# Attention over ragged batches: what the one-tile loops wait for, and how their rows are masked

## The chip, the cores and the metric

The kernel runs on one core of a Trainium2 chip, in one launch. The metric is the device time of that core in microseconds (us). Its engines are named as in the profile: PE (TensorE: matmul, PEld its weight loads), ACT (ScalarE), DVE (VectorE), POOL (GpSimd) and SP (SyncE, which issues the DMAs here). The mean granted TensorE clock of the profiled execution was 0.992 of full speed.

## The reference

For each of 32 batch entries, self-attention with 8 heads of 64 over the first `lengths[b]` rows of 512; the rows behind are zero.

```python
scale = 1.0 / np.sqrt(head_dim)
output = np.zeros_like(x)                       # x: 32 x 512 x 512
for b in range(batch):
    seq_len = lengths[b]                        # 64 to 511
    x_b = x[b, :seq_len].copy()
    q, k, v = np.split(np.matmul(x_b, w_qkv), 3, axis=-1)
    ...                                         # to heads x seq_len x 64
    scores = scale * np.matmul(q, k.transpose(0, 2, 1))
    attn = np.exp(scores - np.max(scores, axis=-1, keepdims=True))
    attn = attn / (np.sum(attn, axis=-1, keepdims=True) + 1e-08)
    output[b, :seq_len] = np.matmul(attn, v).transpose(1, 0, 2).reshape(seq_len, dim)
```

The draw is seeded, so the lengths are always the same. Sorted from longest to shortest they begin with 502, 447, 446, 436 and end with 143, 140, 134, 119, 101, 86, 79, 75.

## The kernel before, in words

**Sorted pairs and twelve loops.** The core sorts the lengths on the chip and works on entries in pairs, longest first: 16 pairs. A pair is one iteration, and its two entries are its two positions, `j` = 0 and 1. There are twelve loops, one for each width N in `LOOPS` (512, 448, and 384 down to 96 in steps of 32), and a pair runs in the loop of the smallest width that holds its longer entry. Two loops have one tile of 128 rows (`n == 1`): width 128 and width 96. With these lengths each of them runs one iteration: pair 14 (101 and 86) in the loop of width 128, pair 15 (79 and 75), the last, in the loop of width 96. The text calls their four positions (14,0), (14,1), (15,0) and (15,1).

**Projections ahead.** A position computes the scores, exponentials, products with the values, and the division of its own entry, and between these the projections Q, K and V of the *next* position's entry, whose transposed rows `xT` a DMA has brought. In the last pair's second position there is no next entry. Its projections and their casts have `skip` set (`ends = int(n == 1 and j == 1)`), and `emit_all` puts them behind a branch: while `pair < B // 2 - skip` they run, otherwise an Else part only raises their semaphores, so that whoever counts on them goes on. So in (14,1) they run, and in (15,1) they are skipped. In both parts `issue` first does the step's waits; in the Else part it then raises the semaphore (L1736) where the engine would have run the step.

**An order written by hand.** `ORDER[N]` lists each position's steps. In a loop of one tile, `S0` are all scores (PE, two banks of PSUM, matmuls of line L1240) and their exponentials (ACT, L1258, two instructions: heads 0 to 3, and heads 4 to 7); `Q0`, `K0`, `V0` are the projections (PE, L290 and L301) with their cast out of PSUM (L1373 and L1389; a `*` puts it on ACT, else it is on DVE); `A0` and `A4` are the products with the values for heads 0 to 3 and 4 to 7 (PE, L1417), each followed by its division (`normed`, DVE). The digits behind `@` are the PSUM banks that the step takes. `L` and `P` write masks of live rows, `D` loads rows, `X` transposes them into `xT`.

**The division.** The products' last column is the sum of the exponentials. `normed` emits three DVE instructions for each of A0 and A4: the reciprocal of the sums (R, L1477), its product with the mask of live rows, taken from the column of `v_aug` (U, L1483), and the product of the 128 x 256 results with it into `out_nat` (O, L1486). The position's store (SP, L1096) waits for both O.

**Waits.** `plan_waits` walks through the steps of a loop in their order, with what was left by the loops before, and gives each step the waits that it needs. `clock[engine]` holds what an engine is known to have seen done; a wait teaches it (`learn`), and a later step of the same engine need not wait for it again. So a wait that a skippable projection makes on PE also serves the steps behind it on PE, in both parts of the branch.

Of the kernel before, what the change touches and what calls it, by code (L numbers as in the profile page):

```python
# [11 lines left out]
FP32 = mybir.dt.float32  # L12
# [3 lines left out]
ALU = mybir.AluOpType  # L16
AX = mybir.AxisListType

P = 128
NH = 8  # L20
HD = 64
# [18 lines left out]
def plan_waits(head, bodies, entries, rare):  # L40
# [22 lines left out]
    def follow(chain):  # L63
# [5 lines left out]
        for at, v in enumerate(chain):  # L69
# [10 lines left out]
            for w, j, k, op in todo:  # L80
                b = -1 if v == "head" else 2 * (at - ahead) + (j or 0)
                mine = clock[op.eng]
                older = w != "head" and came < w - 1

                def learn(o):
# [30 lines left out]
                for o in sorted(needs, key=lambda o: -o["order"]):  # L116
# [3 lines left out]
                    if o["entry"]:  # L120
                        wait = ("entry", o["name"])
                    elif o["name"] not in shared:
                        wait = ("head", o["name"])
                    elif v == "head":
                        wait = ("lead", o["name"])
                    elif before and o["name"] in rare:
                        wait = ("iterin", o["name"], first // 2 - o["b"] // 2)
                    elif o["name"] in rare:
                        wait = ("iter", o["name"], b // 2 - o["b"] // 2)
                    elif o["dma"] and before:  # L130
                        wait = ("iterin", o["name"], first // 2 - o["b"] // 2)
                    elif o["dma"]:
                        wait = ("iter", o["name"], b // 2 - o["b"] // 2)
                    elif o["name"] not in has[v] and (not older or ends_in[o["name"]] < v - 2):
                        wait = ("last", o["name"])
                    elif before:
                        wait = ("posold" if older else "posin", o["name"], first - o["b"])
                    else:
                        wait = ("pos", o["name"], b - o["b"])
# [10 lines left out]
                o = {"name": op.name, "by": by, "count": count, "clock": after, "b": b}  # L150
# [21 lines left out]
def kernel(  # L172
# [8 lines left out]
    nc = tc.nc  # L181
    B, MAXS, D = x.shape
# [6 lines left out]
    const = ctx.enter_context(tc.tile_pool(name="const", bufs=1))  # L189
# [8 lines left out]
    def ring(n, shape, dtype, name, pool=const):  # L198
# [15 lines left out]
    alive = const.tile([P, B + 8, NT], FP32)  # L214

    lasts = const.tile([P, B, NT], FP32)
    queries = const.tile([P, 2, NT], F16)
    spare = const.tile([P, 2], F16)

    last_xT = const.tile([P, NC, 3 * P // 2], F16)  # L220
# [51 lines left out]
    }  # L272

    def steps(N, j):
# [4 lines left out]
    def tiles(N):  # L279
        return -(-N // P)  # L280
# [737 lines left out]
    def position(N, j, at, ring):  # L1018
# [4 lines left out]
        n = tiles(N)  # L1023
        n128 = n * P
        gm = {4: 1, 3: 1, 2: 2, 1: 4}[n]
        heads = {4: 1, 3: 2, 2: 2, 1: 4}[n]
# [4 lines left out]
        o = 1 - j  # L1031
        kT, qz, v_aug, o_t = k_bufs[j], q_bufs[j], v_bufs[j], o_bufs[j]
# [4 lines left out]
        def op(*args, **kw):  # L1037
            ops.append(Op(*args, **kw))
# [35 lines left out]
        def unless_past(ahead, name, transfer):  # L1074

            with nc.If_lt(own_pair, (B - ahead - j + 1) // 2):
                last = transfer()
                if last is not None:
                    last.then_inc(sems[name], 16)
            with nc.Else():  # L1080
                nc.sync.sem_inc(sems[name], unit(name))
            nc.end_ifs()
# [45 lines left out]
        def live(table, t0, t1):  # L1128
# [8 lines left out]
                op0=ALU.add,  # L1137
            )

        def live_queries():  # L1140
            return nc.vector.tensor_scalar(
                out=queries[:, :, 0:n],
                in0=alive[:, bass.ds(at("DVE") + j, 2), 0:n],
                scalar1=0.0,
                scalar2=None,
                op0=ALU.add,
            )
# [324 lines left out]
        def normed(h0):  # L1472
            k, pav = sums[h0]
            rcp = r_bufs[k][:, 0 : heads * n].rearrange("p (g t) -> p g t", t=n)

            def reciprocal():
                return nc.vector.reciprocal(out=rcp, in_=pav[:, :, :, HD])  # L1477

            def only_live():
                rows = v_aug[:, 0:n, h0 : h0 + heads, HD].rearrange("p t g -> p g t")  # L1480
                if half_last:
                    rows = queries[:, 1 - j, 0:n].unsqueeze(1).broadcast_to([P, heads, n])
                return nc.vector.tensor_tensor(out=rcp, in0=rcp, in1=rows, op=ALU.mult)  # L1483

            def divide():
                return nc.vector.tensor_tensor(  # L1486
                    out=o_t[:, 0:n, h0 * HD : (h0 + heads) * HD].rearrange(
                        "p t (g d) -> p g t d", d=HD
                    ),
                    in0=pav[:, :, :, 0:HD],  # L1490
                    in1=rcp.unsqueeze(3).broadcast_to([P, heads, n, HD]),
                    op=ALU.mult,
                )

            op(f"R{h0}", "DVE", reciprocal, (f"bk{k}",), (f"r{k}",))
            whose = f"queries{j}" if half_last else f"vl{j}"
            op(f"U{h0}", "DVE", only_live, (f"r{k}", whose), (f"r{k}",))
            op(f"O{h0}", "DVE", divide, (f"bk{k}", f"r{k}"), (f"o{j}.{h0}",))

        def maybe(name, ahead, transfer):  # L1500
            return transfer if n > 2 else lambda: unless_past(ahead, name, transfer)
# [11 lines left out]
        for step in steps(N, j):  # L1513
            step = step.split("@")[0]
            kind, act = step[0], step.endswith("*")
            if kind in "BU":
                name, engines = step[:2], step[4:]
                if name not in opened:
                    opened[name] = (half_qk if kind == "B" else half_values)(name, int(name[1]))
                opened[name](engines)  # L1520
                continue
            num = int(step.strip("*")[1:] or 0)
            if kind == "P":
                op("M", "DVE", pair_mask, (), (f"m{o}",))
                op(
                    "C",
                    "POOL",
                    casts,
                    (f"xn{o}", f"m{o}"),
                    (f"x16{o}",),  # L1530
                    skip=int(n == 1),
                )
                if half_last and j == 0:
                    for b in (1, 0):
                        op(f"Y{b}", "POOL", lambda b=b: gathered(b), (f"xT{b}",), ("lastT",))
            elif kind == "D":
                op(f"LD{j}", "SP", maybe(f"LD{j}", 5, load), (), (f"xn{o}",), dma=True)
            elif kind == "L" and not half_last:
                op("L", "DVE", lambda: live(alive, 0, n), (), (f"vl{o}",))
            elif kind == "L" and j:  # L1540
                op(
                    "L",
                    "DVE",
                    lambda: (live_queries(), live_lasts(), live(alive, 0, n - 1))[2],
                    (),
                    ("vl0", "vlL", "queries0", "queries1"),
                )
            elif kind == "L":
                op("L", "DVE", lambda: live(alive, 0, n - 1), (), ("vl1",))
            elif kind == "S":  # L1550
                scores(num)
            elif kind in "QK":
                qk(step.strip("*"), num, kind == "Q", act)
            elif kind == "V":
                val(step.strip("*"), num, act)
            elif kind == "A":
                av(num)
            elif kind == "Z":
                rest(num)
            elif kind == "W":  # L1560
                last_values(act)
            elif kind == "X":
                transfer = maybe(f"XT{j}", 3, transposed)
                op(f"XT{j}", "SP", transfer, (f"x16{o}",), (f"xT{o}",), dma=True)
# [58 lines left out]
    def at(eng):  # L1623
        return here[eng]
# [78 lines left out]
    for (v, j, k), todo in waits.items():  # L1703
        op = op_of(v, j, k)
# [35 lines left out]
    def issue(v, j, k, op, instead=None):  # L1740
        eng = EN[op.eng]
        for wait in waits[v, j, k]:
            if wait[0] == "head":
                eng.wait_ge(*point[wait[1]])
                continue
            base, amount = value_of(v, j or 0, wait)
            eng.wait_ge(sems[wait[1]], regs[op.eng][base, amount] if base else amount)
        if (op.eng == "SP" or op.name[0] in "YEZ" or op.ahead) and waits[v, j, k]:
            eng.sem_inc(passed, 1)
        if instead:  # L1750
            return instead()
        here["pads"] = [name for name in op.pads if name in sems]
        last = op.emit()
        if v == "head" and op.name in point:
            last.then_inc(point[op.name][0], 16 if op.dma else 1)
        elif op.name in sems and last is not None:
            last.then_inc(sems[op.name], 16 if op.dma else 1)

    with tc.tile_critical():
# [38 lines left out]
        for v, N in enumerate(LOOPS):  # L1798
# [14 lines left out]
            with nc.body(body):  # L1813
# [4 lines left out]
                p = nc.snap(pair, min_val=0, max_val=B // 2 - 1)  # L1818
                here.update({e: p * 2 for e in EN}, pair=p, pairs=pair)
                for j in range(2):  # L1820
                    for e in EN:
                        mine = [(k, op) for k, op in enumerate(bodies[v][j]) if op.eng == e]
# [54 lines left out]
```

## Time and profile before

| | us |
|---|---|
| median of 3 runs (lowest, highest) | 333.87 (333.55, 335.23) |
| the profiled execution's own time | 334.23 |
| its span, first to last instruction | 332.4 |
| busy in the span: PE / ACT / DVE / POOL | 316.7 / 261.7 / 206.5 / 101.9 |

The profiled execution lies 0.36 us over the median, and 1.8 us of its time lie outside its span. Times in the profile are microseconds from the start of the span. A line such as L1486 is a line of the kernel before. In a row of the timeline stand the start, the duration, the engine, line and operation, what is written from what, a count, and in brackets the engine's idle time before with what ended it. "SPq" or "PEldq" is the engine's sequencer: waits, branches and issues.

### The profile page before, as it was taken

To read this page: it belongs to the slowest core of one execution; us is meant where nothing else is said; L and a number is where in the kernel's file an instruction comes from. 1 tells how busy PE (TensorE), PEld (TensorE's weight loads), DVE (VectorE), ACT (ScalarE), POOL (GpSimd) and SP (SyncE) were. 2 spreads that over 40 slices of the span, in tenths; PEclk is the share of its full clock that TensorE was granted. 3 is DMA by queue.
4 is the path that set the end of the run, shared out by engine and by line. 5 is a ranking of instruction groups with operands and counts; after the bars stand their busy time and mean duration, and the time that the engine had idled before them with its cause. 6 is when DMAs were issued, how large, how long until landed. Compare 5 with 4: busy or idle time off the path is not lost.

```text
span 332.4 us, 12738 instructions
## 1 busy us (share of the span) xinstructions
PE 316.7 (95%) x4800; PEld 202.6 (61%) x4800; DVE 206.5 (62%) x670; ACT 261.7 (79%) x402; POOL 101.9 (31%) x148
## 2 busy tenths in 40 slices
PE   7899999999999999999999999999999999999970
PEld 4444645554665556556556666666778776787750
DVE  6666655676776467466565555564676868656572
ACT  5289899878778987978988899789678687888731
POOL 6537040504030330331232143043222334253310
PEclk9999999999999999999999999999999999999996
DMA  7983999399839997686775777649556666666641
GB/s 220 368 302 65 270 192 299 75 338 224 303 52 336 263 212 223 217 248 217 250 240 187 268 212 224 220 178 284 177 156 168 189 184 197 197 195 226 206 146 64
DMA packets 70709, 71.41 MB, mean 215 GB/s; under 512 B 40704, under 2 KB 40704, under 8 KB 70656
## 3 DMA queue, kind: packets, MB, share of 16 engines
q1 hardware_dynamic: 70608, 70.74, 72.1%
q8 instruction: 29, 0.48, 0.6%
q14 instruction: 24, 0.20, 0.2%
q10 hardware_dynamic: 48, 0.00, 0.0%
HBM read 27.80 MB, written 33.55 MB: 185 GB/s over the span
## 4 chain that ended last, share of the span: by engine, by line
PE 80%; SPq 7%; issue 4%; DVE 3%; DMA 2%; ACT 1%; POOL 0%; ACTq 0%; POOLq 0%
PE banks L1291 42%; PE banks L1417 14%; PE banks L1240 13%; PE banks L301 6%; SPq L318 3%; PE banks L290 3%; DMA x_nat<-in_x_dram 1%; PE banks L1456 1%; DMA xT<-x 1%; DVE rcp L1483 1%; SPq L1085 1%; DVE out_nat L1486 1%; PE banks L1181 1%; ACT et L1258 1%; SPq L1057 1%
## 5 line engine op out<-in xcount | busy, mean ns | idle before, releaser
L1258 ACT ACTIVATE et<-banks 128x704 f16<-128x704 f32 (+8 forms) x256 | 199.4, 823 | 34.6 <-PE banks L1240 31.5
L361 POOL TENSOR_TENSOR x<-x_nat,mask 128x512 f16<-128x512 f32 x83 | 84.2, 1039 | 185.2 <-DVE mask L1041 170.9
L1291 PE MATMUL banks<-xT,w_r 64*128 64x352 f16 (+8 forms) x1536 | 130.5, 299 | 0.4 <-ACT v_aug L1353 0.2
L1291 PEld LDWEIGHTS banks<-xT,w_r 64*128 64x128 f16 x1536 | 69.1, 94 | 38.1 <-PE banks L1291 7.9
L1240 PE MATMUL banks<-qz,kT 64*128 64x352 f16 (+11 forms) x624 | 76.9, 295 | 1.8 <-ACT kT L1373 0.9
L1486 DVE TENSOR_TENSOR out_nat<-banks,rcp 128x256 f32<-128x256 f32 (+1 forms) x136 | 64.1, 471 | 4.8 <-DMA out_dram<-out_nat 0.2
L1417 PEld LDWEIGHTS banks<-v_aug,et 128*128 128x128 f16 x1536 | 52.4, 98 | 19.8 <-issue 10.3
L1417 PE MATMUL banks<-v_aug,et 128*128 128x65 f16 x1536 | 59.4, 194 | 1.5 <-ACT et L1258 1.2
L1334 DVE CAST qz<-banks 128x352 f16<-128x352 f32 (+5 forms) x49 | 28.1, 574 | 41.5 <-PE banks L1291 41.3
L1291 PE MATMUL banks<-w_r,xT 64*128 64x512 f16 x352 | 45.3, 376 | 0.2 <-issue 0.2
L1477 DVE RECIPROCAL rcp<-banks 128x4 f32<-128x4 f32 (+1 forms) x136 | 24.6, 181 | 30.6 <-PE banks L1456 16.9
L1240 PEld LDWEIGHTS banks<-qz,kT 64*128 64x128 f16 x624 | 27.9, 94 | 23.9 <-ACT et L1258 3.2
L1334 DVE CAST kT<-banks 128x448 f16<-128x448 f32 (+5 forms) x47 | 25.8, 558 | 8.2 <-PE banks L1291 8.1
L301 PE MATMUL banks<-w_r,xT 128*128 128x512 f16 x108 | 27.5, 380 | 2.3 <-DMA xT<-x 1.8
L1291 PEld LDWEIGHTS banks<-w_r,xT 64*128 64x128 f16 x352 | 16.3, 94 | 14.3 <-PE banks L1291 1.0
L1353 DVE CAST v_aug<-banks 128x512 f16<-128x512 f32 x21 | 14.1, 691 | 15.9 <-PE banks L1291 15.9
L290 PE MATMUL banks<-xT,w_r 128*128 128x160 f16 (+3 forms) x256 | 23.1, 244 | 0.0
L290 PEld LDWEIGHTS banks<-xT,w_r 128*128 128x128 f16 x256 | 16.9, 98 | 5.0
L1334 ACT CAST qz<-banks 128x352 f16<-128x352 f32 (+5 forms) x31 | 14.7, 476 | 5.1 <-PE banks L1291 4.9
L1483 DVE TENSOR_TENSOR rcp<-rcp,v_aug 128x4 f32<-128x4 f32 (+1 forms) x80 | 15.5, 193 | 2.8
L1334 ACT CAST kT<-banks 128x352 f16<-128x352 f32 (+5 forms) x33 | 16.2, 491 | 0.9 <-PE banks L1291 0.9
L301 PEld LDWEIGHTS banks<-w_r,xT 128*128 128x128 f16 x108 | 8.9, 97 | 12.1 <-issue 2.4
(99 smaller groups left out, 158.0 us busy)
## 6 DMA issues: line engine op xcount, KB each, us to landing
x_nat<-in_x_dram SPq DMA_DIRECT2D x12, 768.0 KB, 6.0
out_dram<-out_nat SPq DMA_DIRECT2D x12, 768.0 KB, 4.5
x_nat<-in_x_dram SPq DMA_DIRECT2D x7, 1024.0 KB, 8.8
x_nat<-in_x_dram SPq DMA_DIRECT2D x13, 512.0 KB, 3.8
out_dram<-zeros SPq DMA_DIRECT2D x12, 512.0 KB, 3.3
out_dram<-out_nat SPq DMA_DIRECT2D x12, 512.0 KB, 4.3
out_dram<-out_nat SPq DMA_DIRECT2D x4, 1024.0 KB, 7.1
out_dram<-zeros SPq DMA_DIRECT2D x4, 768.0 KB, 4.9
```

Of the source, the lines that this page charges most:

```text
L290: last = nc.tensor.matmul(dst[:, 0:N], w_r[:, c, w0 : w0 + P], xT[:, c, 0:N], start=(c == 0), stop=(c == NC - 1),)
L301: last = nc.tensor.matmul(pv, xT[:, c, t * P : (t + 1) * P], w_r[:, c, 2 * D : 3 * D], start=(c == 0), stop=(c == NC - 1),)
L361: return engine.tensor_tensor(out=x16, in0=x32, in1=live.broadcast_to([P, D]), op=ALU.mult)
L1240: last = nc.tensor.matmul(psc[par][:, x * wide : x * wide + N], kT[r, i, c0 : c0 + P], qz[r, i, 0:N], start=True, stop=True,)
L1258: return nc.scalar.activation(out=et[:, :, x0:x1, 0:N], in_=got.rearrange("p j (x q) -> p j x q", q=wide)[:, :, x0:x1, 0:N], func=AF.Exp, ...
L1291: last = nc.tensor.matmul(banks[ks[z]][:, m * width : (m + 1) * width], lhs(rows, c), rhs(rows, c), start=(c == 0 and opens), stop=(c == N ...
L1334: return lambda copy, bank: copy(out=buf[:, ms, 0:N], in_=bank[:, 0 : gm * N].rearrange("p (m q) -> p m q", q=N),)
L1353: return lambda copy, bank: copy(out=v_bufs[o][:, t, :, 0:HD], in_=bank.rearrange("p (h d) -> p h d", d=HD))
L1417: last = nc.tensor.matmul(pav[:, g, qt, :], e_bufs[e][:, c0 + qt * P : c0 + (qt + 1) * P], v_aug[:, kt, h, :], start=(kt == 0 and not (hal ...
L1477: return nc.vector.reciprocal(out=rcp, in_=pav[:, :, :, HD])
L1483: return nc.vector.tensor_tensor(out=rcp, in0=rcp, in1=rows, op=ALU.mult)
L1486: return nc.vector.tensor_tensor(out=o_t[:, 0:n, h0 * HD : (h0 + heads) * HD].rearrange("p t (g d) -> p g t d", d=HD), in0=pav[:, :, :, 0:HD],
```

## The change

In one-tile loops the division no longer takes a masked reciprocal. A [128, 1] scalar `real` says which rows are live; it is written with the other masks, by one more small DVE instruction for each position. O becomes a `scalar_tensor_tensor`: the results times the scalar times the reciprocal. U is gone there. In the Else part of a skipped PE step, `issue` leaves out the waits for casts and exponentials of the same position (names that begin with S or G, at a distance of 0). Because such a step may now have seen less, `plan_waits` gives each skippable PE step a copy of PE's clock, so that what it waits for is not held as known behind it. And the second position of width 96 takes other PSUM banks for K0, V0 and A4.

```diff
             for w, j, k, op in todo:
                 b = -1 if v == "head" else 2 * (at - ahead) + (j or 0)
                 mine = clock[op.eng]
+                if op.skip and op.eng == "PE":
+                    mine = defaultdict(int, mine)
...
+    real = const.tile([P, 2], FP32)
...
-        96: "L P S0@56 Q0*@3 A0@2 K0*@0 A4@7 V0@3 X D | L P S0@45 Q0*@3 K0*@4 V0*@3 X D A0@6 A4@4",
+        96: "L P S0@56 Q0*@3 A0@2 K0*@0 A4@7 V0@3 X D | L P S0@45 Q0*@3 K0*@0 V0*@2 X D A0@6 A4@1",
...
+        def live_rows():
+            return nc.vector.tensor_scalar(
+                out=real[:, j : j + 1],
+                in0=alive[:, bass.ds(at("DVE") + j, 1), 0],
+                scalar1=0.0,
+                scalar2=None,
+                op0=ALU.add,
+            )
...
+            def divide_live():
+                return nc.vector.scalar_tensor_tensor(
+                    out=o_t[:, 0, h0 * HD : (h0 + heads) * HD].rearrange("p (g d) -> p g d", d=HD),
+                    in0=pav[:, :, 0, 0:HD],
+                    scalar=real[:, j : j + 1],
+                    in1=rcp.broadcast_to([P, heads, HD]),
+                    op0=ALU.mult,
+                    op1=ALU.mult,
+                )
+
             op(f"R{h0}", "DVE", reciprocal, (f"bk{k}",), (f"r{k}",))
+            if n == 1:
+                op(f"O{h0}", "DVE", divide_live, (f"bk{k}", f"r{k}", f"real{j}"), (f"o{j}.{h0}",))
+                return
...
+            elif kind == "L" and n == 1:
+                op("L", "DVE", lambda: (live_rows(), live(alive, 0, 1))[1], (), (f"vl{o}", f"real{j}"))
...
     def issue(v, j, k, op, instead=None):
         eng = EN[op.eng]
         for wait in waits[v, j, k]:
+            if instead and op.eng == "PE" and wait[1][0] in "SG" and wait[2:] == (0,):
+                continue
```

## The prediction

> **What bounds the kernel now.** I read the chain's shares first, then busy time by stage, then the chain piece by piece over the last 20 us, because the change reaches only the four one-tile positions.
>
> ```profile
> PE 80%; SPq 7%; issue 4%; DVE 3%; DMA 2%; ACT 1%; POOL 0%; ACTq 0%; POOLq 0%
> ```
> ```profile
> 0.00:311.00 311.00, 305.34 (x4611) 193.85 (x4612) 195.23 (x628) 254.08 (x387) 99.26 (x143) 1.00 0.75 221
> 311.00:323.99 12.99, 10.57 (x176) 8.19 (x175) 8.85 (x34) 6.73 (x14) 2.42 (x4) 1.00 0.51 175
> 323.99:328.04 4.05, 0.76 (x17) 0.52 (x16) 2.37 (x10) 0.87 (x2) 0.20 (x1) 0.88 0.17 66
> 328.04:332.40 4.36, 0.00 (x0) 0.00 (x0) 0.00 (x0) 0.00 (x0) 0.00 (x0) 0.50 0.16 62
> ```
>
> The columns behind the stretch are its length and the busy time of PE, PEld, DVE, ACT and POOL. Up to 311 us PE is busy for 305 of 311 us, in loops of two to four tiles whose instructions the change leaves alone. Pairs 14 and 15 come behind. From 324 us PE works for 0.76 us in 4: this is position (15,1), a chain of single steps. Behind 328 no engine works. So whatever the change gives must come out of some 16 us, and most of it out of the last 4. The chain there, start and duration first:
>
> ```profile
> 312.92 3.87 DMA xT<-x
> ...
> 316.93 1.02 PE banks L301 x4
> ...
> 318.08 1.80 PE banks L290 x32
> ...
> 320.45 0.94 issue
> ...
> 321.54 0.50 ACT et L1258
> ...
> 324.06 0.29 PE banks L1240 x8
> ...
> 324.38 0.07 ACT et L1258
> 324.44 0.32 issue
> 324.76 0.49 ACT et L1258
> 325.25 0.29 issue
> 325.54 0.30 PE banks L1417 x4
> ...
> 325.87 0.19 DVE rcp L1477
> ...
> 326.08 0.17 DVE rcp L1483
> ...
> 326.28 0.42 DVE out_nat L1486
> ...
> 326.83 0.18 DVE rcp L1483
> ...
> 327.03 0.42 DVE out_nat L1486
> ```
>
> The reader is to see two things. A0 of (15,1) (325.54, the first L1417 row) starts 0.29 us behind the end of the *second* exponential, 324.76 + 0.49 = 325.25, though A0 needs only heads 0 to 3, the first. And behind A0 stand five DVE instructions and a store. Why A0 is so late is in the next rows: the three skipped projections' waits on PE (one line of the kernel, seen by source), and the DVE cast that they wait for, with DVE's other rows and the last store from the timeline.
>
> ```profile
> L1736 PEldq EVENT_SEMAPHORE  x3: 51/51/51, 324.8 to 325.4; - x3
> ```
> ```profile
> 324.10 0.69 DVE L1389 CAST v_aug<-banks 128x512 f16<-128x512 f32 x1
> 324.70 0.18 DVE L1129 TENSOR_SCALAR v_aug<-alive 128x8 f16 x1
> 324.77 0.16 DVE L1041 TENSOR_SCALAR mask<-alive 128x4 f32 x1
> ...
> 326.62 0.17 DVE L1477 RECIPROCAL rcp<-banks 128x4 f32<-128x4 f32 x1
> ...
> 327.70 0.33 SPq L1096 DMA_DIRECT2D out_dram<-out_nat  x1
> ```
>
> Q0's wait is answered at 324.8, when V0's cast of (15,0) ends (324.10 + 0.69 = 324.79; Q0 takes that bank). The last of the three waits comes at 325.4. Between them K0 is held: its bank 4 is one that this position's scores fill, so it waits for the second exponential. After 325.25 the rest of the Else part and A0's issue take the 0.29.
>
> **The change, part by part.** *(a) The wait in the Else part.* K0's wait for the exponentials goes, and with banks 0 and 2 for K0 and V0 nothing of this position is left to wait for. What is late next? A0 itself reads the V that the cast writes by 324.79, and Q0 keeps its wait for that cast, which lies one position back (a distance of 1, not 0). So the PE steps start at 324.79 and no earlier. Before, the 0.29 covered K0's and V0's waits and A0's issue; now three skipped waits stand there, and A0, with PE's clock copied, waits for the cast and the first exponential on its own account: two more waits. One costs at least its 0.05 (the row above) and at most half of the 0.29, 0.15. A0 then starts at 324.79 + 0.29 + 2 x (0.05 to 0.15) = 325.18 to 325.38. I take 0.125 for each, near the upper end, as the 0.29 holds two waits with their gaps: **325.33, 0.21 earlier**. The first exponential does not hold it: 324.38 + 0.50 (the length of the same form at 321.54) = 324.88. A4 needs the second, done at 325.25, and comes behind A0.
>
> *(b) U goes, O changes.* Per position two U go; on the path lie only those of (15,1). Each is worth the step from its start to O's: 326.08 to 326.28 and 326.83 to 327.03, 0.20 each, 0.40. In (15,0) the divides end earlier too, but V0's cast behind them starts when V0's matmuls end (324.06 in the chain), so nothing moves. In (14,0) U even costs more:
>
> ```profile
> 314.92 1.04 POOL L361 TENSOR_TENSOR x<-x_nat,mask 128x512 f16<-128x512 f32 x1 [4.66 <-DVE mask L1041]
> ...
> 315.32 0.65 DVE L1483 TENSOR_TENSOR rcp<-rcp,v_aug 128x4 f32<-128x4 f32 x1
> ...
> 317.00 1.22 SPq L318 DMA_TRANSPOSE xT<-x  x1
> ```
>
> It ends at 315.97 as POOL's cast ends (315.96), 0.65 for a 0.17 us operation. This stall goes too, but PE waits for the DMA of 312.92 until 316.93 anyway: worth nothing.
>
> O becomes a `scalar_tensor_tensor` with a pointer scalar over the same 256 elements. The rows nearest to it:
>
> ```profile
> L513 DVE TENSOR_SCALAR h_cmp<-h_key_row,h_key_col x1: 228/228/228, 3.8 to 3.8; 32x32 f32<-32x32 f32 x1
> L494 DVE SCALAR_TENSOR_TENSOR h_key_row<-row,h_idx_f x1: 192/192/192, 3.1 to 3.1; 32x32 f32<-32x32 int32 x1
> L1486 DVE TENSOR_TENSOR out_nat<-banks,rcp 128x256 f32<-128x256 f32 x88 | 37.3, 424 | 3.2 <-DMA out_dram<-out_nat 0.2
> L1486 DVE TENSOR_TENSOR out_nat<-banks,rcp 128x384 f32<-128x384 f32 x48 | 26.8, 557 | 1.6
> ```
>
> With a pointer scalar 32 elements took 0.228, with an immediate in the new form 0.192: the pointer costs about 0.04. [...] A gain is excluded: the element count and operands stay. I take **0.04 for each O, 0.08**, since the rows with the form and with the pointer are the near ones. [...]
>
> *(c) The new mask.* One DVE instruction of 0.16 to 0.18 (the two mask rows at 324.70) for each position. In (15,1) it ends near 325.1, before the reciprocal needs DVE at 325.33 + 0.33 = 325.66; without that cover it would cost its 0.17. In (14,0) it moves POOL's cast from an end of 315.96 to some 316.1; the transposes behind it go out on SP at 317.00, so SP's queue covers it.
>
> *(d) PE's copied clock.* In (14,1) the projections run, and A0, Q0, K0 and A4 must wait again for what V0, Q0 and K0 had seen. These are waits for things long done. PE's idle time ahead of such waits:
>
> ```profile
> L1747 PEldq EVENT_SEMAPHORE  x130: 51/51/718, 22.2 to 322.8; - x130
> L290 PE MATMUL banks<-xT,w_r 128*128 128x160 f16 (+3 forms) x256 | 23.1, 244 | 0.0
> ```
>
> 130 separate waits on PE stand in the span, and the 256 projection matmuls show 0.0 us of idle: the sequencer runs ahead of a filled queue. I take nothing for (d); bounds 0 and 0.15 for each wait that is not covered.
>
> *The sum.* Before, A0's start to the store is 327.70 - 325.54 = 2.16 us. It loses 0.40 and gains 0.08: 1.84. 325.33 + 1.84 = 327.17, against 327.70: **0.53 earlier**. Can SP follow? Its last semaphore step ahead of a store:
>
> ```profile
> L1081 SPq EVENT_SEMAPHORE  x2: 17/17/17, 324.4 to 324.6; - x2
> ...
> L1081 SPq EVENT_SEMAPHORE  x2: 17/17/17, 326.5 to 326.8; - x2
> ...
> 324.91 3.12 SPq L1096 DMA_DIRECT2D out_dram<-out_nat  x2
> ```
>
> The store of (15,0) went out 0.3 behind that step (324.6 to 324.91) with nothing to wait for, so in (15,1) SP allows 327.1: just enough, and no gain above 0.6. What follows the store stays. The profiled execution would take 334.23 - 0.53 = 333.70; it lies 0.36 over the median, and the same 0.53 from 333.87 gives **333.3 us**.
>
> **The rivals.** *Held still (333.55).* The change does not do what it says: some wait that counts as another position's, or A0's own, still holds PE to the second exponential at 325.25. Then A0 stays at 325.54 and only (b) is left, 0.40 - 0.08 = 0.32. For it speaks that only waits at distance 0 go; against it, that banks 0, 2 and 6 carry nothing of this position's scores.
>
> [...]
>
> [...]
>
> *Slower (334.2).* The repeated waits of (d) are not covered. The place is (14,1): from 316.93 (the DMA's landing) to K0's end at 318.08 + 1.80 = 319.88 every PE matmul is on the path. From the fourth exposed wait on (4 x 0.15 = 0.60) they outweigh the 0.53; six give 0.90 - 0.53 = 0.37 slower. The 0.0 us of idle speaks against it; for it, that the queue runs empty while PE waits for that DMA, so that (14,1) starts without a lead.
>
> **How the numbers follow.** Forecast 0.57 (its own range 333.1 to 333.7, from A0 at 325.18 to 325.38, SP's limit, and O's bounds), held still 0.15, half pace 0.10, slower 0.12, code at the edge 0.06. The runs of before lie 0.32 under their median and more above it; the range takes the lowest case less 0.3, and the highest plus 0.2: 332.7 to 334.4. All cases lie within 0.5% (1.67 us, about what a measurement of this kernel can tell from no change); scatter and what I have not seen get 0.05 on each side.
>
> **What would show it.** In the profile after: A0 of (15,1) near 325.3 and before or about the end of the second exponential plus 0.1, with three skipped waits on PE close together; no L1483 rows on `v_aug` with 4 elements behind 315; O at about 0.46; the last store near 327.2; PE in (14,1) without gaps. The prediction is wrong if A0 still starts 0.3 behind the second exponential, if O takes 0.6 or more, or if K0 of (14,1) ends later than some 3 us behind the DMA's landing.

## The result, and the profile after

The changed kernel took 333.16 us (median of 11 runs, 332.44 to 333.62) where the kernel before took 333.92 (11 runs, 333.19 to 335.23). The ratio of all these runs is 0.9968, 95% interval 0.9954 to 0.9982: 1.07 us less, 0.60 to 1.54 (the two medians alone lie 0.76 apart). Two more measurements of it, on two different chips, gave 0.9973 and 0.9981 (below). One of the ten executions of e8_divide96, a kernel below, took 630.24 us and is left out of its ratio. All lie within the 0.5% that the prediction called no change; the time lies 0.14 us under its 333.3.

The profiled execution took 333.01 us with a span of 331.2. Its lines are numbered a little higher: scores L1252, exponentials L1270, products L1429, reciprocal R L1489, the new division O L1508, store L1099, skipped steps' semaphores L1763. First its busy time by stage, columns as in the prediction's table:

```profile
0.00:311.00 311.00, 306.08 (x4614) 194.09 (x4615) 196.18 (x626) 254.25 (x387) 99.23 (x143) 1.00 0.75 220
311.00:323.16 12.16, 10.43 (x174) 8.05 (x171) 8.55 (x33) 6.59 (x14) 2.42 (x4) 1.00 0.58 196
323.16:326.80 3.64, 0.78 (x17) 0.52 (x16) 2.14 (x8) 0.87 (x2) 0.20 (x1) 1.00 0.19 75
326.80:331.20 4.40, 0.00 (x0) 0.00 (x0) 0.00 (x0) 0.00 (x0) 0.00 (x0) 0.62 0.16 61
```

The stages are cut at the same events as before. From the scores of (15,1) to the end of work 4.05 became 3.64; the empty tail stays at about 4.4. The stretch ahead of the scores is 0.83 shorter (12.99, now 12.16), and that one needs care. Here is the chain that ended last, and behind it rows of the timeline:

```profile
324.45 0.13 issue
324.58 0.30 PE banks L1429 x4
324.88 0.02 issue
324.90 0.20 DVE rcp L1489
325.10 0.02 issue
325.12 0.48 DVE out_nat L1508
325.60 0.10 DVE rcp L1489
325.70 0.03 issue
325.73 0.48 DVE out_nat L1508
```
```profile
312.17 1.56 SPq L321 DMA_TRANSPOSE xT<-x  x1
...
314.64 0.15 DVE L1144 TENSOR_SCALAR real<-alive 128x1 f32 x1 [1.13 <-issue]
...
316.11 1.04 PE L304 MATMUL banks<-w_r,xT 128*128 128x512 f16 x4
...
323.29 0.69 DVE L1401 CAST v_aug<-banks 128x512 f16<-128x512 f32 x1 [0.16 <-PE banks L304]
323.57 0.87 ACT L1270 ACTIVATE et<-banks 128x384 f16<-128x384 f32 x2 [0.80 <-PE banks L1252]
323.89 0.14 DVE L1144 TENSOR_SCALAR real<-alive 128x1 f32 x1
...
326.46 0.33 SPq L1099 DMA_DIRECT2D out_dram<-out_nat  x1
```

The chain begins at PE's own issue and no longer at the second exponential: that wait is gone. Two R and two O stand behind A0 (324.58), and no U. From the first exponential of (15,1) to A0 it is 324.58 - 323.57 = 1.01, before 325.54 - 324.38 = 1.16. From A0 to the last store it is 1.88, before 2.16. (Rows are rounded to 0.01; the tables below are worked out from unrounded starts, and have 1.01 and 1.89 here, 1.17 and 2.16 before.)

The two executions differ by 1.2 us in span, and 0.82 of it stands ahead of V0 of (14,1), at 316.93 before and 316.11 after. The transposes that bring its rows were issued at 312.92 before and at 312.17 after. The first instruction that the change adds comes at 314.64, so it can't have moved them. Ahead of them on SP stands the load of the next pair's word from a table in memory. It ended 0.2 us before the issue in both, but took 1.57 us in one trace and 0.28 in the other (by source; first before, then after; nanoseconds, then the start):

```profile
L1057 SPq TENSOR_LOAD <-table x1: 1565/1565/1565, 311.1 to 311.1; - x1
```
```profile
L1060 SPq TENSOR_LOAD <-table x1: 284/284/284, 311.7 to 311.7; - x1
```

In the 14 profiled executions of this study V0 of (14,1) starts anywhere from 315.76 to 317.56 us, with either division. A comparison of two spans would credit the change with this. Only distances between events behind it can be compared, and the times of many runs.

### The profile page after: what moved, and what is told of

The parts are those of the page before. It is cut to its first block, busy times and chain, and to the rows that moved or that the text cites. A ratio compares the mean times of both kernels' runs of the same rounds, so it can differ in the third digit from the quotient of the medians.

```text
span 331.2 us, 12738 instructions
## 1 busy us (share of the span) xinstructions
PE 317.3 (96%) x4800; PEld 202.7 (61%) x4800; DVE 206.9 (62%) x666; ACT 261.7 (79%) x402; POOL 101.8 (31%) x148
## 5 line engine op out<-in xcount | busy, mean ns | idle before, releaser
L1270 ACT ACTIVATE et<-banks 128x704 f16<-128x704 f32 (+8 forms) x256 | 199.5, 823 | 35.3 <-PE banks L1252 32.1
L1252 PE MATMUL banks<-qz,kT 64*128 64x352 f16 (+11 forms) x624 | 77.0, 295 | 2.4 <-DVE out_nat L1508 0.9
L1429 PEld LDWEIGHTS banks<-v_aug,et 128*128 128x128 f16 x1536 | 52.4, 97 | 19.6 <-issue 8.9
L1498 DVE TENSOR_TENSOR out_nat<-banks,rcp 128x256 f32<-128x256 f32 (+1 forms) x128 | 60.7, 474 | 4.6 <-DMA out_dram<-out_nat 0.3
L1429 PE MATMUL banks<-v_aug,et 128*128 128x65 f16 x1536 | 59.4, 194 | 1.4 <-ACTq L1763 1.1
L1489 DVE RECIPROCAL rcp<-banks 128x4 f32<-128x4 f32 (+1 forms) x136 | 24.6, 181 | 30.6 <-PE banks L1468 16.6
L1252 PEld LDWEIGHTS banks<-qz,kT 64*128 64x128 f16 x624 | 27.9, 94 | 24.7 <-ACT et L1270 3.2
L1495 DVE TENSOR_TENSOR rcp<-rcp,v_aug 128x4 f32<-128x4 f32 (+1 forms) x72 | 13.9, 193 | 2.5
```

The source lines that it names most:

```text
L1252: last = nc.tensor.matmul(psc[par][:, x * wide : x * wide + N], kT[r, i, c0 : c0 + P], qz[r, i, 0:N], start=True, stop=True,)
L1270: return nc.scalar.activation(out=et[:, :, x0:x1, 0:N], in_=got.rearrange("p j (x q) -> p j x q", q=wide)[:, :, x0:x1, 0:N], func=AF.Exp, ...
L1429: last = nc.tensor.matmul(pav[:, g, qt, :], e_bufs[e][:, c0 + qt * P : c0 + (qt + 1) * P], v_aug[:, kt, h, :], start=(kt == 0 and not (hal ...
L1498: return nc.vector.tensor_tensor(out=o_t[:, 0:n, h0 * HD : (h0 + heads) * HD].rearrange("p t (g d) -> p g t d", d=HD), in0=pav[:, :, :, 0:HD],
```

## The experiments

All are measured in these distances, worked out from rows of each kernel's timeline, and in a ratio to the kernel before, timed on the same chip. "V0 to exp" runs from V0 of (14,1) to the first exponential of (15,0), "exp" alone is the first exponential of (15,1). The last column is the ratio less one, times the median of before (333.9 to 334.2).

| kernel | V0 to exp | exp to A0 | A0 to store | exp to store | ratio (95%) | us |
|---|---|---|---|---|---|---|
| before | 4.61 | 1.17 | 2.16 | 3.33 | | |
| after | 4.63 | 1.01 | 1.89 | 2.90 | 0.9968 (0.9954 to 0.9982) | -1.07 |
| e1_before | 4.87 | 1.17 | 2.17 | 3.33 | 0.9995 (0.9979 to 1.0010) | -0.17 |
| e2_divide | 4.62 | 1.16 | 1.89 | 3.05 | 0.9986 (0.9969 to 1.0002) | -0.47 |
| e3_wait | 4.87 | 1.01 | 2.17 | 3.18 | 0.9985 (0.9969 to 1.0002) | -0.50 |
| e4_banks | 4.61 | 0.95 | 2.17 | 3.12 | 0.9989 (0.9973 to 1.0004) | -0.37 |
| e5_after_again | 4.62 | 1.01 | 1.89 | 2.90 | 0.9973 (0.9957 to 0.9989) | -0.90 |
| e6_divide_banks | 4.61 | 0.86 | 1.89 | 2.75 | 0.9977 (0.9959 to 0.9996) | -0.77 |
| e7_divide128 | 4.62 | 1.17 | 2.17 | 3.33 | 0.9998 (0.9978 to 1.0019) | -0.07 |
| e8_divide96 | 4.61 | 1.17 | 1.89 | 3.06 | 0.9994 (0.9971 to 1.0016) | -0.20 |
| e9_best | 4.61 | 0.56 | 1.97 | 2.53 | 0.9974 (0.9958 to 0.9990) | -0.87 |
| e10_after_third | 4.62 | 1.01 | 1.89 | 2.90 | 0.9981 (0.9964 to 0.9998) | -0.63 |
| e11_a0_first | 4.61 | 0.56 | 2.16 | 2.72 | 0.9968 (0.9952 to 0.9983) | -1.07 |
| e12_u_pointer | 4.61 | 1.16 | 2.30 | 3.46 | one time, 334.41 us | |

**The two parts apart.** The first four ran on one chip: the kernel before again, the division alone, the waits alone (with the other banks), and the other banks alone.

The kernel before, once more, no edit:

> The kernel before, once more, against itself. Every theory: ratio 1.000, its interval about 0.997 to 1.003 wide. What is looked at is the trace: from the start of (15,1)'s first exponential to the last store 3.32 us as in the first trace (324.38 to 327.70), with a scatter below 0.1; and the start of that exponential, 324.38 there. Theory 'local' (the change acts behind (15,1)'s scores alone, 0.43 us, and the rest of the measured 1.07 is scatter of what comes before) says that this start moves by some 0.5 us between executions of the same kernel, for example with the landing of the transposed rows for (14,1) at 316.80. Theory 'upstream' (the change also shortens the way to that start) says that it stays near 324.4.

The division alone (with the change's `real`, `live_rows` and `divide_live`):

```diff
+            if n == 1:
+                op(f"O{h0}", "DVE", divide_live, (f"bk{k}", f"r{k}", f"real{j}"), (f"o{j}.{h0}",))
+                return
```

> The kernel before with the new division alone (the scalar of live rows, no masked reciprocal in one-tile loops). Theory 'local': A0 of (15,1) still starts 0.29 behind the second exponential; from the first exponential to the store 3.32 - 0.40 + 0.12 = 3.04 us; ratio 0.9992 (0.28 us faster). Theory 'upstream, by the masked reciprocals that stand still behind GpSimd's casts': most of the 1.07 us is here, ratio 0.9972 to 0.998, and (15,1)'s exponential starts some 0.6 us earlier than in the kernel before.

PE's copied clock, the left-out waits, and the banks, with the division of before:

```diff
+                if op.skip and op.eng == "PE":
+                    mine = defaultdict(int, mine)
...
-        96: "L P S0@56 Q0*@3 A0@2 K0*@0 A4@7 V0@3 X D | L P S0@45 Q0*@3 K0*@4 V0*@3 X D A0@6 A4@4",
+        96: "L P S0@56 Q0*@3 A0@2 K0*@0 A4@7 V0@3 X D | L P S0@45 Q0*@3 K0*@0 V0*@2 X D A0@6 A4@1",
...
+            if instead and op.eng == "PE" and wait[1][0] in "SG" and wait[2:] == (0,):
+                continue
```

> The kernel before with the other half alone: the waits of the skipped part, the copied clock and the new banks, and the old division. Theory 'local': A0 of (15,1) starts 1.01 us behind the first exponential's start instead of 1.16; to the store 3.32 - 0.15 = 3.17 us; ratio 0.9995. Theory 'upstream, by the waits': ratio 0.998 or lower. The price of the repeated waits in (14,1) shows too: from the first matmul of V0 to the end of K0's in (14,1) 2.95 us in the kernel before; every exposed wait adds up to 0.15.

The banks alone:

```diff
-        96: "L P S0@56 Q0*@3 A0@2 K0*@0 A4@7 V0@3 X D | L P S0@45 Q0*@3 K0*@4 V0*@3 X D A0@6 A4@4",
+        96: "L P S0@56 Q0*@3 A0@2 K0*@0 A4@7 V0@3 X D | L P S0@45 Q0*@3 K0*@0 V0*@2 X D A0@6 A4@1",
```

> The kernel before with the new banks of width 96 alone; waits are planned and issued as before. If it is the shared bank that held K0 and V0 in the skipped part, nothing of this position is left to wait for, and A0 of (15,1) starts about as early as with the whole change or earlier, since A0 need not repeat its waits: 0.9 to 1.0 us behind the first exponential's start; ratio 0.9994. If leaving out the waits is what matters, A0 stays at 1.16.

The division takes 0.28 off the stretch behind A0 and leaves A0 where it was. The wait part takes 0.15 off the stretch ahead of A0 and leaves the rest. 0.28 + 0.15 = 0.43 is what the changed kernel shows (3.33 to 2.90) in each of its three traces. The banks alone release A0: in the chain of e2_divide, which has the old banks, A0 still starts 0.28 behind the second exponential (first block), and in that of e4_banks (second block) the second exponential is gone from the chain (the ACT row there is the first), without copied clock or left-out wait:

```profile
323.61 0.49 ACT et L1268
324.10 0.28 issue
324.38 0.30 PE banks L1427 x4
```
```profile
325.00 0.50 ACT et L1258
325.50 0.46 issue
325.95 0.30 PE banks L1417 x4
```

So with K0 and V0 in banks 0 and 2 the rule that leaves waits out gave A0 nothing more: it is at 0.95 without that rule and the copied clock, at 1.01 with them.

The times of the two parts, 0.9986 and 0.9985, are too close to 1 to tell either from no change alone.

**The kernel before has two courses in pair 14.** Its second trace, e1_before, took 4.87 from V0 to the first exponential of (15,0), not 4.61, and so did e3_wait, the other kernel with the old U there. The timeline of e1_before:

```profile
318.75 1.04 POOL L361 TENSOR_TENSOR x<-x_nat,mask 128x512 f16<-128x512 f32 x1 [1.46 <-DVE mask L1041]
...
319.39 0.42 DVE L1483 TENSOR_TENSOR rcp<-rcp,v_aug 128x4 f32<-128x4 f32 x1
...
319.85 0.42 DVE L1486 TENSOR_TENSOR out_nat<-banks,rcp 128x256 f32<-128x256 f32 x1
...
320.19 0.68 DVE L1373 CAST qz<-banks 128x512 f16<-128x512 f32 x1
...
321.45 0.35 PE L1240 MATMUL banks<-qz,kT 64*128 64x96 f16 x8 [0.81 <-DVE qz L1373]
```

U stalls here in (14,1) too, until POOL's cast ends (318.75 + 1.04 = 319.79; U ends at 319.81). O and Q0's cast on DVE come late, and the bracket of the last row names DVE's cast as what the scores of (15,0) waited for, 0.81. In before's trace the DMA came so late that the division of (14,0) was over when it landed: U at 315.32, 1.6 us ahead of V0. In e1_before U of (14,0) began at 316.66, 0.3 ahead of V0 at 316.96; its stall of 0.66 put off what DVE does behind it, the mask and hence POOL's next cast too, and U of (14,1) then lay under that cast.

Sorted by when the rows land, all traces agree. In seven they are in time, and V0 starts 0.05 behind the start of the first exponential of (14,1): e1_before and e3_wait, with the old U in pair 14, show 4.87, and the five without it (after, e2_divide, e5_after_again, e7_divide128, e10_after_third) 4.62 to 4.63. In the other seven V0 starts 0.7 to 1.4 behind that exponential, and they show 4.61 with either division. Of the five traces with the old U in pair 14 (before, e1_before, e3_wait, e4_banks, e8_divide96) two show 4.87 and three 4.61. So the change also removes 0.26 from some executions, 0.1 on the mean over these five.

**What the copied clock costs, and the division loop by loop.** On the second chip: after again, division and banks without the copied clock, the division in the loop of width 128 alone, and in that of width 96 alone.

The changed kernel, no edit:

> The changed kernel once more. 'Local' (0.43 us behind (15,1)'s exponential and nothing else): ratio 0.9987, and a first measurement of 0.9968 that lay low by scatter. 'Local and the stalled reciprocals' (0.43, and up to 0.26 from the start of V0 in (14,1) to (15,0)'s exponential, where before took 4.61 or 4.87 us): ratio 0.998; 4.62 us in that stretch, 2.90 us from (15,1)'s exponential to the store.

The edit of e2_divide and that of e4_banks together:

> The kernel before with the new division and the new banks of width 96, without the copied clock and without leaving out waits. If the banks alone release A0 of (15,1), and the copied clock only costs A0 a wait of its own, it starts 0.95 us behind the first exponential (1.01 in the changed kernel, 1.16 before), and from there to the store 2.84 us against 2.90 and 3.33; ratio 0.9984 or, with the stalls, 0.9978. If the left-out waits carry the gain, A0 stays at 1.16 and the stretch at 3.05.

The division in pair 14 alone, the step U kept there as one that only raises its semaphore:

```diff
+            if N == 128:
+                step = lambda name=f"U{h0}": (name in sems and nc.vector.sem_inc(sems[name], 1), None)[1]
+                op(f"U{h0}", "DVE", step, (f"r{k}",), (f"r{k}",))
+                op(f"O{h0}", "DVE", divide_live, (f"bk{k}", f"r{k}", f"real{j}"), (f"o{j}.{h0}",))
+                return
```

> The new division in the loop of width 128 alone (pair 14); width 96 keeps the masked reciprocal. Where it stood, an empty step raises its semaphore. 'Local': nothing that matters changes, 3.33 us from (15,1)'s exponential to the store, ratio 1.000. 'Stalled reciprocals': 4.61 to 4.65 us from V0 of (14,1) to (15,0)'s exponential whether the transposed rows come early or late; ratio 0.9992 to 1.000.

The division in pair 15 alone:

```diff
+            if N == 96:
+                op(f"O{h0}", "DVE", divide_live, (f"bk{k}", f"r{k}", f"real{j}"), (f"o{j}.{h0}",))
+                return
```

> The new division in the loop of width 96 alone (pair 15); pair 14 keeps the masked reciprocal and its stalls. 'Local': 3.05 us from (15,1)'s exponential to the store, ratio 0.9992. 'Stalled reciprocals': the same 3.05, and where V0 of (14,1) starts before about 316.9 us in the span less than 0.1 us behind its position's exponential, 4.87 us from there to (15,0)'s exponential, because the second masked reciprocal of pair 14 stands still behind GpSimd's cast and delays Q0's cast; 4.61 where the rows land later.

Without the copied clock A0 starts at 0.86 instead of 1.01: the wait that it makes PE repeat ahead of A0 costs 0.15 here. The chain of e6_divide_banks:

```profile
323.42 0.50 ACT et L1268
323.92 0.36 issue
324.27 0.30 PE banks L1427 x4
```

e4_banks, also without the copy, had 0.95: its skipped waits stand 0.1 further apart in one trace, which stays unexplained. All of the 0.28 behind A0 is in the loop of width 96 (e8_divide96); the division in width 128 (e7_divide128) changes nothing behind (15,1)'s exponential and has only the stall of pair 14 to give. Its time, 0.9998 (0.9978 to 1.0019), can't show 0.1.

Its trace shows something else. The step left in U's place takes DVE about as long as an unstalled U, and the rows land in time:

```profile
317.99 0.17 DVE L1487 RECIPROCAL rcp<-banks 128x4 f32<-128x4 f32 x1
318.39 0.48 DVE L1506 SCALAR_TENSOR_TENSOR out_nat<-banks,real,rcp 128x256 f32<-128x256 f32 x1 [0.23 <-DVEq L1517]
```

R to O is 0.40 here, 0.41 at this place in before (318.60 to 319.01), and V0 to the exponential is 4.62. So the 0.26 is the price of the stalls and not of U's plain time.

**How far this goes.** On the third chip: a version made from what the runs pointed to, after a third time, the same without its SP part, and the cheaper-looking other way to do U. e9_best is e6_divide_banks with A0 ahead of the skipped steps, so that it passes none of their waits, and with SP's load of the next pair's word (`N`) behind the store instead of ahead of it:

```diff
-        96: "L P S0@56 Q0*@3 A0@2 K0*@0 A4@7 V0@3 X D | L P S0@45 Q0*@3 K0*@4 V0*@3 X D A0@6 A4@4",
+        96: "L P S0@56 Q0*@3 A0@2 K0*@0 A4@7 V0@3 X D | L P S0@45 A0@6 Q0*@3 K0*@0 V0*@2 X D A4@1",
...
-            if j:
+            if j and n > 1:
...
+        if j and n == 1:
+            op("N", "SP", following)
```

> A version meant to beat both: the new division and banks, no copied clock and no left-out waits, A0 ahead of the skipped projections in width 96, and the load of the next pair's word (SP, 0.53 us between the last two stores) put behind the store in one-tile loops. A0 then waits for the cast and the first exponential only, and starts 0.5 us behind that exponential's start (0.86 in the kernel with the division and the banks); from there to the store 2.4 us against 2.75, 2.90 in the changed kernel and 3.33 before. Ratio to before: 0.9973 if only this stretch counts (0.93 us), 0.996 if the excess that the changed kernel showed twice (measured 0.9968 and 0.9973 against 0.9987 from the stretch) is real.

> The changed kernel a third time, for the excess alone. 'Scatter': 0.9984 (0.43 us behind the last exponential and on average 0.1 from the stalls). 'Something more upstream': 0.997 again.

e11_a0_first has the first of these three changes, not the other two:

> The same as the version meant to beat both, but SP's load stays between the last two stores. If SP sets the end there, A0 starts as early (0.5 behind the exponential) and the store does not: 2.65 to 2.75 us from the exponential to the store, as without A0's new place. If DVE sets it, 2.4.

A0 now starts 0.07 behind the exponential that it needs, in both kernels. In e11_a0_first SP is late instead; rows of its timeline, and its load by source:

```profile
326.17 0.48 DVE L1506 SCALAR_TENSOR_TENSOR out_nat<-banks,real,rcp 128x256 f32<-128x256 f32 x1
327.07 0.33 SPq L1097 DMA_DIRECT2D out_dram<-out_nat  x1
```
```profile
L1058 SPq TENSOR_LOAD <-table x1: 542/542/542, 325.6 to 325.6; - x1
```

The store goes out 0.42 behind the end of O (326.65). In the changed kernel it is 0.25 (325.73 + 0.48 to 326.46), and in e9_best, with the load moved behind the store, 0.24:

```profile
325.69 0.29 PE L1427 MATMUL banks<-v_aug,et 128*128 128x65 f16 x4 [0.42 <-ACT et L1268]
326.02 0.18 DVE L1487 RECIPROCAL rcp<-banks 128x4 f32<-128x4 f32 x1
326.23 0.48 DVE L1506 SCALAR_TENSOR_TENSOR out_nat<-banks,real,rcp 128x256 f32<-128x256 f32 x1
326.95 0.33 SPq L1097 DMA_DIRECT2D out_dram<-out_nat  x1
```

What is late there is A4: it stands behind the three skipped steps (325.69, though the second exponential ended at 324.81 + 0.48 = 325.29), its reciprocal starts when O of A0 is already done (326.00), and A0 to the store is 1.97, not 1.89. e9_best is 0.80 shorter than before behind the exponential and 0.37 shorter than after. Its time does not show the 0.37: 0.9974 against 0.9981 for the changed kernel on that chip, with intervals that hold each other's value. A4 ahead of the skipped steps as well was not tried.

e12_u_pointer keeps U and the old O, and takes U's factor from the scalar instead of a second tensor:

```diff
+                rows = r_bufs[k][:, 0:heads]
+                return nc.vector.tensor_scalar(
+                    out=rows, in0=rows, scalar1=real[:, j : j + 1], scalar2=None, op0=ALU.mult
+                )
```

> The kernel before, but in one-tile loops U multiplies the reciprocal by the [128, 1] scalar through a pointer instead of by a second tensor; O is as before. What it tells is why U stood still behind GpSimd's cast in (14,0) (0.65 to 0.67 us instead of 0.17). If two SBUF tensors are the cause, U with one tensor and a pointer takes 0.17 to 0.22 there; if any operation from SBUF to SBUF stands still, it still ends with the cast. Behind (15,1)'s exponential it changes nothing: 3.33 to 3.40 us to the store.

```profile
315.38 1.04 POOL L362 TENSOR_TENSOR x<-x_nat,mask 128x512 f16<-128x512 f32 x1 [4.39 <-DVE mask L1042]
...
316.01 0.44 DVE L1518 TENSOR_SCALAR rcp<-rcp,real 128x4 f32<-128x4 f32 x1
...
317.03 0.23 DVE L1518 TENSOR_SCALAR rcp<-rcp,real 128x4 f32<-128x4 f32 x1
...
318.01 1.04 POOL L362 TENSOR_TENSOR x<-x_nat,mask 128x512 f16<-128x512 f32 x1 [1.59 <-DVE mask L1042]
...
318.81 0.41 DVE L1518 TENSOR_SCALAR rcp<-rcp,real 128x4 f32<-128x4 f32 x1
```

With one tensor and a pointer U still stalls behind POOL's cast (316.01 + 0.44 = 316.45, the cast ended at 316.42) and takes 0.23 where nothing stalls it, against 0.17 before. A0 to the store became 2.30, 0.14 longer than before. So a pointer instead of the second tensor cures neither the stall nor the time; taking U away does.

## Why the prediction was right, and where not

**The waits (a).** Forecast 0.21, measured 0.15. A0 was to start 0.54 behind the end of V0's cast (0.29 and two waits of 0.125); it starts 0.60 behind it (324.58, the cast ended at 323.29 + 0.69 = 323.98). The three skipped waits stand close together as forecast:

```profile
L1763 PEldq EVENT_SEMAPHORE  x3: 51/51/51, 324.0 to 324.3; - x3
```

The prediction added two steps to its 0.29 for A0's own two waits, at 0.125 each. Two steps were added, but not these. The 0.29 of before holds K0's and V0's steps; Q0's is the third above and comes on top. And of A0's own waits only one stands as a step of its own in the trace of after, a row that e6_divide_banks, without the copied clock, doesn't have:

```profile
L1776 PEldq EVENT_SEMAPHORE  x1: 51/51/51, 324.5 to 324.5; - x1
```

Each of the two costs 0.15 (the three steps above stand that far apart, and e6_divide_banks starts A0 0.15 earlier): 0.29 + 2 x 0.15 = 0.59, against the 0.60 measured. So the count came out right by luck, and the price of a step lay at the upper bound of the prediction. That K0 was held through bank 4 was right, and e4_banks shows that this alone mattered. The prediction did not separate the banks from the left-out waits, and so didn't see that the banks without the copied clock give more.

**The division (b).** U's 0.40 came as forecast. O is the term mis-sized within it, 0.06 for each and not 0.04:

```profile
L1508 DVE SCALAR_TENSOR_TENSOR out_nat<-banks,real,rcp x8: 482/484/485, 315.8 to 325.7; 128x256 f32<-128x256 f32 x8
```

0.484 against 0.424. So A0 to the store lost 0.28 and not 0.32. Together with (a) the stretch behind the exponential lost 0.43 where 0.53 was forecast.

**The stall in (14,0), "worth nothing".** This step failed. It rested on one trace, in which PE waited for the DMA until 316.93. Where the DMA comes early against the division, U's stall runs on into (14,1), on to Q0's cast and the scores of (15,0): 0.26 in two of five traces. With 0.1 on the mean the sum is again 0.53, but by luck: what (a) and (b) fell short of and what was put at nothing cancel.

**The mask (c) and the copied clock in (14,1) (d).** Right. The new mask's 0.14 at 323.89 is over long before R at 324.90, and V0 to the first exponential of (15,0) is 4.61 to 4.63 with and without the copied clock, and 4.87 with it (e3_wait) as without (e1_before) where the old U stalls.

**SP's limit.** Right: it was put at 0.6. With 0.58 gained (e6_divide_banks) the store goes out 0.25 behind the end of O (325.43 + 0.48 to 326.16), as in the changed kernel; in e11_a0_first it is late by 0.17 and the gain stops at 0.61.

**The rivals.** Held still is refuted by A0's place, and slower by (d). Half pace (0.10 among the chances, and O's upper bound) stands on a pace of O that no run shows: the new O, with one tensor from PSUM, one from SBUF and the pointer from SBUF, takes 0.484, the old one 0.424. Code at the loop's edge (0.06, and with 333.0 the lowest case of the range) stands on a link between the length of the code and ACT's pause ahead of the first exponential of (15,0), which no run shows either. The pause stayed: ACT is idle for 1.05 ahead of that exponential in before and in after, and the chain of e2_divide has:

```profile
319.29 0.94 issue
```

**What stays open.** The three measurements of the changed kernel (-1.07, -0.90, -0.63 us) have a mean of -0.87; taken as independent, an estimate of its interval is -1.17 to -0.57. The traces account for 0.53: 0.43 each time, 0.1 from the stall. That lies just outside. But other ratios miss their own distances by as much, with 0.1 counted where pair 14 has no U: e1_before, in which nothing was changed, reads 0.17 too much, e3_wait 0.35 and e11_a0_first 0.36, while e7_divide128, e8_divide96 and e9_best read 0.03 to 0.08 too little. And no trace shows a place for the 0.3: the starts of V0 in (14,1), which scatter by 1.8 us, would hide it. Whether the change also moves these starts, the runs do not settle. So the forecast time was met to 0.14 us although the first ratio gives twice the forecast gain; the 11 executions of each kernel spread over 1.2 and 2 us, and a hit this close is in part luck. Most marks of the prediction were given as absolute times (A0 near 325.3, store near 327.2), and against 324.58 and 326.46 they can't be read because of that scatter; they should have been distances from an event ahead of them. The one that was a distance can: A0 was to start at the latest about 0.1 behind the end of the second exponential, and starts 0.14 behind it (324.58, against 323.57 + 0.87 = 324.44).

## What to carry to other kernels

A skipped step still waits for its PSUM bank: give it one that the work around it doesn't use, and this may do all that a rule for leaving out waits was meant to do, without its repeated waits. A stall that is covered in one trace is covered only as long as the transfer beside it is that late, so look at a second execution of the same kernel before costing it at nothing. And for a gain of some tenths, measure distances between events behind the last scattering transfer, not spans.

## What the runs showed of the hardware that was not expected

SP's load of a single word ahead of the transposes for (14,1) took between 0.28 us (after) and 1.67 (e6_divide_banks) at the same place, and the transposes behind it were issued 0.2 us after its end in before and in after.

In the one-tile loops U took longer on DVE where POOL's cast ran beside it: with two tensors 0.42 to 0.67 us against 0.17 elsewhere, and in the pointer form 0.44 and 0.41 against 0.23. The new O, which reads the products from PSUM, did not: the two beside a cast (315.81 and 318.00) took 0.48 like the other six. In the changed kernel:

```profile
317.19 1.04 POOL L364 TENSOR_TENSOR x<-x_nat,mask 128x512 f16<-128x512 f32 x1 [0.96 <-DVE mask L1044]
...
318.00 0.48 DVE L1508 SCALAR_TENSOR_TENSOR out_nat<-banks,real,rcp 128x256 f32<-128x256 f32 x1
```

O starts under the cast (which ends at 318.23) and takes its 0.48. Both forms of U read and write SBUF alone, O reads one tensor from PSUM; which difference decides it, no run here shows. A pointer is not needed for it: the `tensor_scalar` of L1129, with an immediate and one SBUF tensor, took longer too. In before:

```profile
22.08 3.05 POOL L361 TENSOR_TENSOR x<-x_nat,mask 128x512 f16<-128x512 f32 x3 [5.12 <-DMA x_nat<-in_x_dram]
...
22.70 0.51 DVE L1129 TENSOR_SCALAR v_aug<-alive 128x32 f16 x1
...
42.57 0.23 DVE L1129 TENSOR_SCALAR v_aug<-alive 128x32 f16 x1
```

The first ends at 23.21, 0.09 behind the end of the first of three casts of about 1.04 (22.08 + 1.04 = 23.12). It takes 0.51 here and 0.72 at the same place in after, against 0.23 at 42.57 here, and again 0.23 at 42.28 in after, where no cast runs.
